# A transformer layer with 32 experts on one core: the maxima's transposes move to another PSUM room, VectorE gets a written order in the attention, and TensorE a written order with five batches of transposes in the experts

## The chip, the core and the metric

The kernel runs on one core of one Trainium2 chip. The metric is the device time of one execution in microseconds (us); of several executions the median is compared. Engines are TensorE (PE in the profile, with PEld for its weight loads), VectorE (DVE), ScalarE (ACT), GpSimd (POOL) and SyncE (SP, which issues most DMAs here).

## What is computed

One layer on a sequence of 1024 positions and width 1024: grouped-query attention (16 query heads of 64, 4 key/value heads, so four query heads share a group), then LayerNorm, then a mixture of 32 experts of which each token takes four, then LayerNorm.

```python
def query_block(q_blk):                       # 128 queries
    s = jnp.einsum('bqkgd,bskd->bkgqs', q_blk, k).astype(jnp.float32) * scale
    p = jax.nn.softmax(s, axis=-1).astype(v.dtype)
    return jnp.einsum('bkgqs,bskd->bqkgd', p, v)
...
def clamped_swiglu(h):
    h_glu = jnp.minimum(h[..., 0::2], SWIGLU_LIMIT)
    h_lin = jnp.clip(h[..., 1::2], -SWIGLU_LIMIT, SWIGLU_LIMIT)
    return h_glu * jax.nn.sigmoid(SWIGLU_ALPHA * h_glu) * (h_lin + 1.0)
...
def expert_block(args):                       # 128 rows of one expert
    xblk, e = args
    h = xblk @ w_gate_up[e] + b_gate_up[e]
    return clamped_swiglu(h) @ w_down[e] + b_down[e]
...
x = layer_norm(DEEPNORM_ALPHA * x + h, ln_mix_g[i], ln_mix_b[i])
f = moe_ffn(x, ...)                           # top 4 of 32, weighted by gates
x = layer_norm(DEEPNORM_ALPHA * x + f, ln_ffn_g[i], ln_ffn_b[i])
```

## The kernel before, in words

Everything is in 32-bit floats. A product that must be exact is made from a high and a low part of its operands: ScalarE casts the high part, VectorE subtracts it from the whole to get the low part, and TensorE adds three products.

**Attention.** The loop has 32 iterations n, of a query block i (0 to 7) and a group g (0 to 3), n = 4i + g, and in each eight steps k over blocks of 128 keys. In one step TensorE makes the transposed scores of its own iteration in two matmuls (`st<-qs,kT_hi` and `st<-q,kT_lo`), which ScalarE turns into `pt` by exp, and one matmul `sc` of the scores of iteration n + 2, of which only the maxima are wanted: VectorE reduces each pair of them (`nm<-sc`). Those four columns of negative maxima are transposed by TensorE (`tpm`, in `maxima_a`) and multiplied by VectorE into four rows of the operand `q2` (`q<-tpm,ident`), so that the second `st` matmul subtracts the maxima; ScalarE copies the rest of that operand (`maxima_b`). At k = 3 TensorE also makes the values' product of iteration n - 1 (`po`, 32 narrow matmuls, in `pv`). GpSimd adds up six of the eight `pt` of an iteration (`acc`), VectorE the last (`late_sum`). In iterations g = 1 and 2 the next block's queries are transposed in front of `po` (`tpq`, in `stack_q`, with two casts by ScalarE and two subtractions by VectorE). Once a block the sums are brought together (`su`), VectorE takes the reciprocal and spreads it (`rs`, `rh`, `rr`, all in `scale_a`), and two matmuls `rb` with two multiplications `ot<-ot,rb` scale the block's result (`scale_b`).

In PSUM `st` and `sc` have two rooms each, `po` one (`ps_o`), and all of `tpm`, `tpq`, `su` and `rb` share one (`ps_t`, tag `tp`): whoever writes it next waits until the one before has been read. TensorE runs in the order in which the code is written (`manual_schedule`); VectorE, ScalarE and GpSimd get their order from a scheduler when the kernel is built. Each engine runs its own list from front to back.

**Experts.** Expert e has eight gate/up chunks of 12 matmuls (`gu`, in `gate_up(e)`) and then the four down chunks of the expert before (`yp`, in `down(e-1)`). Each chunk's weights come by DMA, are cast by ScalarE (`wh`) and subtracted by VectorE (`wl`), in three rooms each: the cast of a chunk starts when TensorE has read the chunk three before it. Eighteen experts (1 to 8, and the even ones from 10 to 28) have room for 32 more rows: `go` in two batches of 32 matmuls, after chunk 3 and chunk 7, and `yq` at the end of the down product. Between chunks TensorE transposes what the next products need: `tpa` (two batches of four) and `tpao` (two transposes) for the down product of expert e - 1, and `tpx` (two batches of four) and `tpxo` (two) for expert e + 1, through one PSUM room again (`tp`); ScalarE and VectorE read it out (`xTh`, `xTl`, `aTh`, `aTl`, `xoT`, `aoT`). After `gate_up(e)` the activation is made: VectorE two `act<-gu`, ScalarE the silu, VectorE two `lin<-gu` and one `act<-lin,act`. Matmuls that only open a product with the bias (`gu<-b,sel`, `go<-b,sel`) depend on no weights. Only inside the down product of an expert with extra rows is TensorE's order the written one; elsewhere the scheduler may move its work. The loop that places the transposes:

```python
if e > 0:
    for part in range(3):
        between[part] = lambda part=part: turn_a(e - 1, part)
if e + 1 < NE:
    ...
        for part in range(3):
            between[(4 if e == 2 else 3) + part] = lambda part=part: turn_x(e + 1, part)
```

## Time and profile before

| | |
|---|---|
| time, three runs | 2078.68, 2079.25, 2081.83 us; median 2079.25 us |
| the profiled execution | 2075.34 us, of which the span from first to last instruction is 2073.5 us |
| granted TensorE clock, mean | 0.991 |
| busy share of the span | PE 97%, DVE 77%, ACT 62%, POOL 26% |
| stages of the span (us) | attention's loop 162.1 to 514.8; experts 633.5 to 2029.3 |

Busy shares are means over stages with different limits. TensorE is near its full share in both stages, so what a change is worth shows in TensorE's waits there, and in those that the change adds. An instruction's duration contains its start-up and write-out, so neighbours on one engine overlap a little; the distance from start to start is what it costs the engine.

### The profile page before, as it was taken

To read this page: it belongs to the slowest core of one execution; us is meant where nothing else is said; L and a number is where in the kernel's file an instruction comes from. 1 tells how busy PE (TensorE), PEld (TensorE's weight loads), DVE (VectorE), ACT (ScalarE), POOL (GpSimd) and SP (SyncE) were. 2 spreads that over 40 slices of the span, in tenths; PEclk is the share of its full clock that TensorE was granted. 3 is DMA by queue.
4 is the path that set the end of the run, shared out by engine and by line. 5 is a ranking of instruction groups with operands and counts; after the bars stand their busy time and mean duration, and the time that the engine had idled before them with its cause. 6 is when DMAs were issued, how large, how long until landed. Compare 5 with 4: busy or idle time off the path is not lost. (4 is left out here: it accounts for less than half of the span.)

```text
span 2073.5 us, 28716 instructions
## 1 busy us (share of the span) xinstructions
PE 2011.8 (97%) x10691; PEld 1419.5 (68%) x10691; DVE 1601.8 (77%) x1649; ACT 1282.0 (62%) x1566; POOL 538.2 (26%) x373
## 2 busy tenths in 40 slices
PE   8998999999997999999999999999999999999997
PEld 6775666665675666666666767767777677677774
DVE  6647777776887877767777878878878788887894
ACT  5655655654554656566666766667667676676774
POOL 1216777775144211111102111101021121010100
PEclk9999999999998999999999999999999999999999
DMA  5216000000645777888788898978989889789875
GB/s 174 72 62 178 31 32 21 32 21 21 228 149 211 276 287 271 298 294 291 285 315 312 347 338 304 377 289 342 338 319 354 310 315 367 284 346 337 329 314 183
DMA packets 106352, 500.44 MB, mean 241 GB/s; under 512 B 16001, under 2 KB 17026, under 8 KB 73442
## 3 DMA queue, kind: packets, MB, share of 16 engines
q1 hardware_dynamic: 87360, 447.02, 56.0%
q0 software_dynamic: 16000, 50.90, 9.0%
q8 instruction: 85, 1.39, 0.3%
q10 hardware_dynamic: 2850, 0.66, 0.2%
q14 instruction: 57, 0.47, 0.1%
HBM read 457.05 MB, written 41.49 MB: 240 GB/s over the span
## 5 line engine op out<-in xcount | busy, mean ns | idle before, releaser
L55 PE MATMUL gu<-wh,xTh 128*128 128x512 f32 x1024 | 415.3, 406 | 1.0 <-ACT xTh L63 1.0
L55 PE MATMUL gu<-wh,xTl 128*128 128x512 f32 x1024 | 410.1, 400 | 0.0
L55 PE MATMUL gu<-wl,xTh 128*128 128x512 f32 x1024 | 401.9, 393 | 0.0
L1299 POOL DMA_INDIRECT fd<-y,mi x32 | 79.1, 2472 | 655.4 <-ACT y L1298 655.4
L448 POOL TENSOR_TENSOR acc<-acc,pt 128x512 f32<-128x512 f32 x152 | 211.8, 1394 | 78.3 <-ACT pt L444 68.7
L55 PEld LDWEIGHTS gu<-wh,xTh 128*128 128x128 f32 x1024 | 193.3, 189 | 42.4 <-ACT xTh L63 1.7
L55 PEld LDWEIGHTS gu<-wl,xTh 128*128 128x128 f32 x1024 | 193.3, 189 | 39.6 <-issue 0.2
L55 PEld LDWEIGHTS gu<-wh,xTl 128*128 128x128 f32 x1024 | 193.7, 189 | 38.8 <-issue 3.6
L55 PE MATMUL yp<-wl,aTh 128*128 128x512 f32 x512 | 204.2, 399 | 0.4 <-DVE wl L612 0.4
L55 PE MATMUL yp<-wh,aTh 128*128 128x512 f32 x512 | 201.6, 394 | 0.0
L55 PE MATMUL yp<-wh,aTl 128*128 128x512 f32 x512 | 199.7, 390 | 0.0
L434 DVE TENSOR_REDUCE nm<-sc 128x1 fp32r<-128x1024 f32 x124 | 150.6, 1221 | 50.5 <-PE sc L55 49.5
L444 ACT ACTIVATE pt<-st 128x512 f32<-128x512 f32 x256 | 149.4, 596 | 55.9 <-PE st L55 46.3
L598 POOL DMA_INDIRECT xg<-xd,mi x32 | 53.4, 1670 | 298.5 <-PE tpx L1136 288.9
L55 PE MATMUL qkv<-wh,xT 128*128 128x512 f32 x384 | 123.9, 403 | 2.6 <-ACT xT L63 1.4
L55 PEld LDWEIGHTS yp<-wh,aTh 128*128 128x128 f32 x512 | 96.2, 188 | 33.6 <-ACT act L1180 14.3
L55 PE MATMUL po<-pt,vn 128*64 128x256 f32 x1024 | 117.6, 382 | 0.0
L55 PE MATMUL st<-qs,kT_hi 128*128 128x512 f32 x256 | 112.5, 440 | 2.9 <-ACT pt L444 2.2
L55 PEld LDWEIGHTS yp<-wl,aTh 128*128 128x128 f32 x512 | 96.3, 188 | 21.9 <-DVE wl L612 1.2
L55 PEld LDWEIGHTS yp<-wh,aTl 128*128 128x128 f32 x512 | 96.1, 188 | 19.5
L55 PE MATMUL st<-q,kT_lo 128*128 128x512 f32 x256 | 102.2, 399 | 1.3 <-DVE q L148 1.3
L55 PE MATMUL sc<-kT_hi,qs 128*128 128x512 f32 x256 | 101.9, 404 | 1.0 <-DVE nm L434 0.8
(520 smaller groups left out, 4159.0 us busy)
## 6 DMA issues: line engine op xcount, KB each, us to landing
w0g<-in_expert_w_gate_up SPq DMA_DIRECT2D x8, 1024.0 KB, 7.1
w1g<-in_expert_w_gate_up SPq DMA_DIRECT2D x8, 1024.0 KB, 7.6
w2g<-in_expert_w_gate_up SPq DMA_DIRECT2D x8, 1024.0 KB, 9.6
w3g<-in_expert_w_gate_up SPq DMA_DIRECT2D x8, 1024.0 KB, 8.6
w4g<-in_expert_w_gate_up SPq DMA_DIRECT2D x8, 1024.0 KB, 6.9
w5g<-in_expert_w_gate_up SPq DMA_DIRECT2D x8, 1024.0 KB, 7.4
w6g<-in_expert_w_gate_up SPq DMA_DIRECT2D x8, 1024.0 KB, 6.5
w7g<-in_expert_w_gate_up SPq DMA_DIRECT2D x8, 1024.0 KB, 7.1
```

Of the source, the lines that this page charges most:

```text
L55: nc.tensor.matmul(o, lhsT=lhsT, rhs=rhs, start=start, stop=stop)
L434: nc.vector.tensor_reduce(nms[n][:, m:m + 1], sc.pop((n, m)), AX.X, ALU.max, negate=True)
L444: nc.scalar.activation(pts[n, k], st, AF.Exp)
L448: (nc.vector if n == NG - 1 or n == NG - 2 and k > 3 else nc.gpsimd).tensor_tensor(accs[n], pts[n, 0] if k == 1 else accs[n], pts[n, k], A ...
L598: return nc.gpsimd.indirect_dma_start(out=xg[e], out_offset=None, in_=xd, in_offset=bass.IndirectOffsetOnAxis(ap=mi[:, e:e + 1] if rows is ...
L1299: nc.gpsimd.indirect_dma_start(out=fd, out_offset=bass.IndirectOffsetOnAxis(ap=mi[:, e:e + 1], axis=0), in_=y, in_offset=None, bounds_chec ...
```

## The change

*Attention.* `tpm` is written into the room of the values (`ps_o`, tag `po`, of which `po` now takes half), and from iteration 1 on at k = 5 rather than k = 2. `late_sum` stands behind `stack_q` and `maxima_b`. The multiplication `rr` leaves `scale_a` and becomes `scale_c`, at k = 7 of g = 0. `scale_b` moves from g = 1 (k = 5 and 7) to g = 3 (k = 1 and 5) of the same block. VectorE too runs in the written order in this loop.

*Experts.* From after `gate_up(1)` to the end TensorE runs in the written order. The transposes stand behind chunks 0 and 2 (`tpa`), 4 (new `turn_o`: `tpxo` and `tpao` as one batch in one room) and 5 and 7 (`tpx`), rather than 0, 1, 2 and 3, 4, 5. The bias of `go` is opened just before its first batch.

```diff
-    def maxima_a(n, ps):
-
-        tp = ps.tile([P, 4, P], F32, tag="tp", name=f"tpm{n}")
+    def maxima_a(n, tp):
+
...
         def pv(n):
...
-            po[n] = ps_o.tile([P, 2, P], F32, tag="po", name=f"po{n}")
+            po[n] = ps_o.tile([P, 4, P], F32, tag="po", name=f"po{n}")
...
             nc.vector.scalar_tensor_tensor(rs, hi.bitcast(F32), low, rs, ALU.mult, ALU.subtract)
+            rrs[i] = rs
+
+        def scale_c(i):
+            rs = rrs[i]
...
-        pe_order.enter_context(tc.manual_schedule(engines={mybir.EngineType.PE}))
+        pe_order.enter_context(tc.manual_schedule(engines={mybir.EngineType.PE, mybir.EngineType.DVE}))
...
-                if k == (6 if n == 0 else 2) and n + 1 < NG:
-                    maxima_a(n + 1, ps_t)
+                if k == (6 if n == 0 else 5) and n + 1 < NG:
+
+                    maxima_a(n + 1, ps_o.tile([P, 4, P], F32, tag="po", name=f"tpm{n + 1}"))
...
-                if k == (7 if n == 0 else 3) and n + 1 < NG:
+                if n == 0 and k == 7:
                     maxima_b(n + 1)
+                if k == 7 and g == 0 and 0 < n < NG:
+                    scale_c(i - 1)
                 if k == 3 and n > 0:
                     if g in (1, 2) and i + 1 < NT:
                         stack_q(i + 1, g - 1, ps_t)
+                    if n + 1 < NG:
+                        maxima_b(n + 1)
                     if n < NG - 1:
                         late_sum(n - 1)
...
-                    if (g, k) == (1, 5) or n == NG and k == 5:
+                    if (g, k) == (3, 1) or n == NG and k == 5:
                         scale_b(i - 1, 0)
-                    if (g, k) == (1, 7) or n == NG and k == 7:
+                    if (g, k) == (3, 5) or n == NG and k == 7:
                         scale_b(i - 1, 1)
...
+        def turn_o(e):
+
+            tp = ps_t.tile([P, 4, P], F32, tag="tp", name=f"tpo{e}")
+            if e + 1 < NE and ovf(e + 1):
+                for c in range(2):
+                    nc.tensor.transpose(tp[:, 2 + c, :], xo[e + 1][:, c * P:(c + 1) * P], ident)
+                xoT[e + 1] = mp.tile([P, 2, P], F32, tag="xoT", bufs=2, name=f"xoT{e + 1}")
+                nc.scalar.copy(xoT[e + 1], tp[:, 2:4, :])
+            if ovf(e - 1):
+                for c in range(2):
+                    nc.tensor.transpose(tp[:, c, :], acto[e - 1][:, c * P:(c + 1) * P], ident)
+                nc.scalar.copy(actoT[e - 1], tp[:, 0:2, :])
...
-            for n in range(4 if ovf(e) else 0):
-                mm(go[n * OVF:(n + 1) * OVF], sel[:, e:e + 1].to_broadcast([P, OVF]),
-                   b3[:, n * 512:(n + 1) * 512], True, False)
...
                 if k % 4 == 4 - 1:
+                    for n in range(4 if ovf(e) and k == 4 - 1 else 0):
+                        mm(go[n * OVF:(n + 1) * OVF], sel[:, e:e + 1].to_broadcast([P, OVF]),
+                           b3[:, n * 512:(n + 1) * 512], True, False)
...
-            in_turn = ExitStack()
-            if ovf(e):
-                in_turn.enter_context(tc.manual_schedule(engines={mybir.EngineType.PE}))
...
+            elif e > 1:
+                between[0] = lambda: turn_a(e - 1, 0)
+                between[2] = lambda: turn_a(e - 1, 1)
+                between[4] = lambda: turn_o(e)
...
-                    for part in range(3):
-                        between[(4 if e == 2 else 3) + part] = lambda part=part: turn_x(e + 1, part)
+                    for k, part in zip((5, 7) if e > 1 else (3, 4, 5), range(3)):
+                        between[k] = lambda part=part: turn_x(e + 1, part)
...
             if e == 1:
                 list_blocks()
+
+                in_turn.enter_context(tc.manual_schedule(engines={mybir.EngineType.PE}))
```

How the rows stand on the engines, before and after, at three places. Names carry numbers here: `sc23_1` is the second score matmul pair of iteration 23, `acc22` the sums of iteration 22.

TensorE in the attention, iteration 21 (block 5, g = 1), steps 2 and 3, before:

```order
L147 MATMUL tpm22_3692<-ident_70,nm22_3577 4x128
L55 MATMUL st21_2_3695<-qs5_3305,kT_hi_105 128x512
L55 MATMUL st21_2_3695<-q2_0_112,kT_lo_106 128x512
L55 MATMUL sc23_1_3701<-kT_hi_105,qs5_3305 128x512
L55 MATMUL st21_3_3703<-qs5_3305,kT_hi_105 128x512
L55 MATMUL st21_3_3703<-q2_0_112,kT_lo_106 128x512
L55 MATMUL sc23_1_3701<-kT_hi_105,qs5_3305 128x512
L163 MATMUL tpq6_0_3713<-ident_70,ql6_3666 128x128 x4
L55 MATMUL po20_3725<-pt20_0_3565,vn_107 64x256 x2
```

TensorE in the same iteration, step 4's end to step 6, with the change:

```order
L55 MATMUL sc23_2_3747<-kT_hi_105,qs5_3301 128x512
L146 MATMUL tpm22_3749<-ident_70,nm22_3577 4x128
L55 MATMUL st21_5_3752<-qs5_3301,kT_hi_105 128x512
L55 MATMUL st21_5_3752<-q2_0_112,kT_lo_106 128x512
L55 MATMUL sc23_2_3747<-kT_hi_105,qs5_3301 128x512
L55 MATMUL st21_6_3760<-qs5_3301,kT_hi_105 128x512
```

The transpose `tpm22` has left the place ahead of step 2, where the room is then taken by `tpq6_0`, and stands between steps 4 and 5, behind the values' product.

VectorE at the end of block 5's first iteration (n = 20) and into the next, before:

```order
L452 TENSOR_TENSOR acc23_3885<-acc23_3885,pt23_7_3963 128x512
L434 TENSOR_REDUCE nm26_3982<-sc26_0_3973 128x1
L148 TENSOR_TENSOR q2_1_1558<-tpm25_3984,ident_70 4x512
L434 TENSOR_REDUCE nm26_3982<-sc26_1_3993 128x1
L479 RECIPROCAL rs5_4040<-su5_4023 128x128
L481 CAST rh5_4042<-rs5_4040 128x128
L482 SCALAR_TENSOR_TENSOR rs5_4040<-rh5_4042,low_122,rs5_4040 128x128
L434 TENSOR_REDUCE nm26_3982<-sc26_2_4053 128x1
L484 TENSOR_TENSOR rr5_4045<-rs5_4040,col_120 128x1024
L434 TENSOR_REDUCE nm26_3982<-sc26_3_4069 128x1
L434 TENSOR_REDUCE nm27_4095<-sc27_0_4086 128x1
```

The same stretch with the change (`late_sum` is `acc23`, the reciprocal's chain `rs5`, `rh5`, `rr5`):

```order
L433 TENSOR_REDUCE nm26_3982<-sc26_0_3973 128x1
L433 TENSOR_REDUCE nm26_3982<-sc26_1_3990 128x1
L451 TENSOR_TENSOR acc23_3878<-acc23_3878,pt23_7_3963 128x512
L478 RECIPROCAL rs5_4037<-su5_4020 128x128
L480 CAST rh5_4039<-rs5_4037 128x128
L481 SCALAR_TENSOR_TENSOR rs5_4037<-rh5_4039,low_122,rs5_4037 128x128
L147 TENSOR_TENSOR q2_1_1558<-tpm25_4050,ident_70 4x512
L433 TENSOR_REDUCE nm26_3982<-sc26_2_4048 128x1
L433 TENSOR_REDUCE nm26_3982<-sc26_3_4067 128x1
L487 TENSOR_TENSOR rr5_4078<-rs5_4037,col_120 128x1024
L433 TENSOR_REDUCE nm27_4095<-sc27_0_4086 128x1
```

The multiplication into `q2` has moved behind the reciprocal's chain, `late_sum` behind the two reductions, and `rr5` behind the last reduction of the iteration.

VectorE around the end of the gate/up product of expert 15, which has no extra rows (`wl184` to `wl187` are the four down chunks of expert 14; `xTl_16` comes from the transposes `tpx16`), before:

```order
L64 TENSOR_TENSOR xTl_16_11546<-tpx16_0_11548,xTh_16_11545 128x512
L612 TENSOR_TENSOR wl183_11584<-w15g7_11394,wh183_11582 128x2048
L64 TENSOR_TENSOR xTl_16_11546<-tpx16_1_11573,xTh_16_11545 128x512
L612 TENSOR_TENSOR wl184_11606<-w14d0_11412,wh184_11604 128x2048
L1179 TENSOR_SCALAR act15_11440<-gu15_0_11434 128x512
L612 TENSOR_TENSOR wl185_11624<-w14d1_11442,wh185_11622 128x2048
L1179 TENSOR_SCALAR act15_11440<-gu15_1_11435 128x512
L1183 TENSOR_SCALAR lin15_11441<-gu15_0_11434 128x512
L1183 TENSOR_SCALAR lin15_11441<-gu15_1_11435 128x512
L612 TENSOR_TENSOR wl186_11657<-w14d2_11470,wh186_11655 128x2048
L1185 SCALAR_TENSOR_TENSOR act15_11440<-lin15_11441,act15_11440 128x1024
L612 TENSOR_TENSOR wl187_11675<-w14d3_11495,wh187_11673 128x2048
```

VectorE at the same place with the change:

```order
L622 TENSOR_TENSOR wl184_11564<-w14d0_11378,wh184_11562 128x2048
L64 TENSOR_TENSOR xTl_16_11552<-tpx16_0_11553,xTh_16_11551 128x512
L1202 TENSOR_SCALAR act15_11406<-gu15_0_11400 128x512
L622 TENSOR_TENSOR wl185_11582<-w14d1_11408,wh185_11580 128x2048
L1202 TENSOR_SCALAR act15_11406<-gu15_1_11401 128x512
L64 TENSOR_TENSOR xTl_16_11552<-tpx16_1_11596,xTh_16_11551 128x512
L1206 TENSOR_SCALAR lin15_11407<-gu15_0_11400 128x512
L1206 TENSOR_SCALAR lin15_11407<-gu15_1_11401 128x512
L622 TENSOR_TENSOR wl186_11620<-w14d2_11436,wh186_11618 128x2048
L1208 SCALAR_TENSOR_TENSOR act15_11406<-lin15_11407,act15_11406 128x1024
L622 TENSOR_TENSOR wl187_11638<-w14d3_11454,wh187_11636 128x2048
```

The first `xTl_16` now stands behind `wl184` and the second behind both `act15`, ahead of `lin15`, `wl186` and `wl187`.

ScalarE at the same place, before:

```order
L63 CAST xTh_16_11545<-tpx16_0_11548 128x512
L607 CAST wh183_11582<-w15g7_11394 128x2048
L63 CAST xTh_16_11545<-tpx16_1_11573 128x512
L607 CAST wh184_11604<-w14d0_11412 128x2048
L1138 COPY xoT16_11547<-tpxo16_11598 128x256
L607 CAST wh185_11622<-w14d1_11442 128x2048
L607 CAST wh186_11655<-w14d2_11470 128x2048
L1180 ACTIVATE act15_11440<-act15_11440 128x1024
L607 CAST wh187_11673<-w14d3_11495 128x2048
```

ScalarE with the change:

```order
L617 CAST wh183_11535<-w15g7_11360 128x2048
L1187 COPY xoT16_11528<-tpo15_11525 128x256
L1191 COPY aoT14_11428<-tpo15_11525 128x256
L617 CAST wh184_11562<-w14d0_11378 128x2048
L63 CAST xTh_16_11551<-tpx16_0_11553 128x512
L617 CAST wh185_11580<-w14d1_11408 128x2048
L617 CAST wh186_11618<-w14d2_11436 128x2048
L63 CAST xTh_16_11551<-tpx16_1_11596 128x512
L1203 ACTIVATE act15_11406<-act15_11406 128x1024
L617 CAST wh187_11636<-w14d3_11454 128x2048
```

The second cast `xTh_16` now stands behind the cast `wh186`, and the copies `xoT16` and `aoT14` follow each other.

## Rows read from the trace of the kernel before

**Rows 1.** Busy time by stretch: the attention's steady part, experts 4 to 28.

```profile
core 0: us, PE busy (x) PEld busy (x) DVE busy (x) ACT busy (x) POOL busy (x), PEclk, DMA share, GB/s
...
201.00:497.00 296.00, 284.70 (x1826) 185.39 (x1826) 229.24 (x228) 171.54 (x307) 223.64 (x163) 1.00 0.09 32
...
820.00:1949.00 1129.00, 1129.00 (x5931) 799.70 (x5930) 902.47 (x613) 740.71 (x536) 167.34 (x80) 1.00 0.85 320
```

**Rows 2.** TensorE's waits, 201 to 497 us: total, times, longest.

```profile
PE tpq L163 <- DVE q L148: 4.1, 12, 0.5
PE tpm L147 <- DVE nm L434: 3.9, 7, 0.6
PE rb L55 <- DVE ot L492: 2.7, 7, 0.4
```

**Rows 3.** TensorE's waits, 160 to 201 us.

```profile
PE tpq L163 <- DVE q L148: 3.2, 2, 2.8
```

**Rows 4.** Busy time by stretch: the four iterations of block 5.

```profile
386.92:397.81 10.89, 10.89 (x91) 7.16 (x90) 8.82 (x10) 5.44 (x10) 7.99 (x7) 1.00 0.01 2
397.81:410.13 12.32, 11.12 (x65) 7.27 (x64) 10.31 (x11) 8.09 (x15) 9.98 (x7) 1.00 0.01 1
410.13:420.90 10.77, 10.25 (x62) 6.68 (x61) 7.66 (x9) 6.69 (x12) 7.08 (x7) 1.00 0.28 99
420.90:430.92 10.02, 9.96 (x58) 6.41 (x58) 7.25 (x6) 5.55 (x10) 7.99 (x7) 1.00 0.01 2
sum 44.00, PE 42.22 PEld 27.51 DVE 34.06 ACT 25.77 POOL 33.05; mean PE 10.55 PEld 6.88 DVE 8.51 ACT 6.44 POOL 8.26
```

**Rows 5.** Timeline of VectorE in block 5's first iteration: start, duration.

```profile
389.55 1.76 DVE L452 TENSOR_TENSOR acc<-acc,pt 128x512 f32<-128x512 f32 x1 [1.20 <-POOL acc L448]
...
392.48 0.68 DVE L148 TENSOR_TENSOR q<-tpm,ident 4x512 fp32r<-4x512 f32 x1
...
394.94 0.96 DVE L479 RECIPROCAL rs<-su 128x128 f32<-128x128 f32 x1 [0.53 <-PE su L55]
...
396.51 1.22 DVE L434 TENSOR_REDUCE nm<-sc 128x1 fp32r<-128x1024 f32 x1
397.65 1.21 DVE L484 TENSOR_TENSOR rr<-rs,col 128x1024 fp32r<-128x1024 f32 x1
```

**Rows 6.** Timeline of TensorE, block 5's second iteration into its third.

```profile
406.09 0.50 PE L55 MATMUL st<-qs,kT_hi 128*128 128x512 f32 x1
...
406.89 0.40 PE L55 MATMUL st<-qs,kT_hi 128*128 128x512 f32 x1
...
410.13 0.39 PE L55 MATMUL st<-qs,kT_hi 128*128 128x512 f32 x1
...
410.83 0.39 PE L55 MATMUL st<-qs,kT_hi 128*128 128x512 f32 x1
```

**Rows 7.** Timeline of VectorE, expert 15's activation and expert 14's down weights.

```profile
1347.76 0.68 DVE L1179 TENSOR_SCALAR act<-gu 128x512 f32<-128x512 f32 x1
1348.36 1.28 DVE L1183 TENSOR_SCALAR lin<-gu 128x512 f32<-128x512 f32 x2
1349.55 2.28 DVE L612 TENSOR_TENSOR wl<-w14d,wh 128x2048 fp32r<-128x2048 f32 x1
1351.75 1.22 DVE L1185 SCALAR_TENSOR_TENSOR act<-lin,act 128x1024 f32<-128x1024 f32 x1
1352.89 2.28 DVE L612 TENSOR_TENSOR wl<-w14d,wh 128x2048 fp32r<-128x2048 f32 x1
```

**Rows 8.** Timeline of ScalarE, the same stretch.

```profile
1339.41 0.59 ACT L63 CAST xTh<-tpx 128x512 fp32r<-128x512 f32 x1 [0.46 <-PE tpx L1136]
...
1342.41 0.37 ACT L1138 COPY xoT<-tpxo 128x256 f32<-128x256 f32 x1 [0.16 <-PE tpxo L1136]
...
1346.08 1.91 ACT L607 CAST wh<-w14d 128x2048 fp32r<-128x2048 f32 x1 [0.82 <-PE gu L55]
```

**Rows 9.** Timeline of TensorE, the same stretch: transposes between chunks and inside one.

```profile
1333.63 0.39 PE L55 MATMUL gu<-wl,xTh 128*128 128x512 f32 x1
1333.87 0.60 PE L1136 MATMUL tpx<-ident,xg 128*128 128x128 f32 x4
...
1334.53 0.40 PE L55 MATMUL gu<-wh,xTl 128*128 128x512 f32 x1
...
1338.43 0.39 PE L55 MATMUL gu<-wh,xTh 128*128 128x512 f32 x1
...
1339.45 0.40 PE L55 MATMUL gu<-wl,xTh 128*128 128x512 f32 x1
```

**Rows 10.** Timeline of TensorE, expert 14's down product.

```profile
1346.11 0.39 PE L55 MATMUL yp<-wh,aTh 128*128 128x512 f32 x1
...
1351.77 0.39 PE L55 MATMUL yp<-wh,aTl 128*128 128x512 f32 x1
...
1352.04 0.58 PE L55 MATMUL yp<-wl,aTh 128*128 128x512 f32 x1
```

More of the change, by code (lines that the diff above doesn't have):

```diff
@@ L348, in trunk_kernel @@
                 if i == NT - 1 and k == 6:
-                    maxima_a(0, ps1)
+                    maxima_a(0, ps1.tile([P, 4, P], F32, tag="tp", name="tpm0"))
                     maxima_b(0)
@@ L456, in pv @@
             i, g = divmod(n, NKV)
-            po[n] = ps_o.tile([P, 2, P], F32, tag="po", name=f"po{n}")
+            po[n] = ps_o.tile([P, 4, P], F32, tag="po", name=f"po{n}")
             for k in range(NT):
                 for a in range(2):
-                    mm(po[n][a * HD:(a + 1) * HD].rearrange("p j t -> p (j t)"), vn[:, k, g, :],
+                    mm(po[n][a * HD:(a + 1) * HD, 0:2, :].rearrange("p j t -> p (j t)"), vn[:, k, g, :],
                        pts[n, k][:, 2 * a * P:(2 * a + 2) * P], k == 0, k == NT - 1)
@@ L468, in close_a @@
                 ot[i] = p2.tile([P, KD, P], F32, tag="ot", bufs=2, name=f"ot{i}")
-            nc.scalar.copy(ot[i][:, 2 * g:2 * g + 2, :], po.pop(n))
+            nc.scalar.copy(ot[i][:, 2 * g:2 * g + 2, :], po.pop(n)[:, 0:2, :])
         def scale_a(i):
@@ L553, in trunk_kernel @@
                         scale_a(i - 1)
+                    if n == NG:
+                        scale_c(i - 1)
                 if i > 0:
-                    if (g, k) == (1, 5) or n == NG and k == 5:
+                    if (g, k) == (3, 1) or n == NG and k == 5:
                         scale_b(i - 1, 0)
-                    if (g, k) == (1, 7) or n == NG and k == 7:
+                    if (g, k) == (3, 5) or n == NG and k == 7:
                         scale_b(i - 1, 1)
@@ L1144, in turn_x @@
                 xT[e] = [mx.tile([P, KD, P], F32R, tag=f"xT{a}", bufs=2, name=f"xT{a}_{e}") for a in "hl"]
-                if ovf(e):
+                if ovf(e) and e < 3:
                     xoT[e] = mp.tile([P, 2, P], F32, tag="xoT", bufs=2, name=f"xoT{e}")
@@ L1269, in down @@
             later = []
-            in_turn = ExitStack()
-            if ovf(e):
-                in_turn.enter_context(tc.manual_schedule(engines={mybir.EngineType.PE}))
             for c in range(KD // 2):
@@ L1296, in down @@
                     between[c]()
-            in_turn.close()
             nc.scalar.mul(y, yp, gm_s[:, e:e + 1])
@@ L1318, in trunk_kernel @@
         fetch(8)
+        in_turn = ExitStack()
         for e in range(NE):
             between = {}
-            if e > 0:
+            if e == 1:
                 for part in range(3):
                     between[part] = lambda part=part: turn_a(e - 1, part)
+            elif e > 1:
+                between[0] = lambda: turn_a(e - 1, 0)
+                between[2] = lambda: turn_a(e - 1, 1)
+                between[4] = lambda: turn_o(e)
             if e + 1 < NE:
@@ L1344, in trunk_kernel @@
         down(NE - 1)
+        in_turn.close()
     es_w.close()
```

## The prediction, made before the changed kernel ran

> **What bounds the kernel now.** I read the busy time by stretch first. From 820 to 1949 us, in the middle of the experts, TensorE is busy for 1129.00 of 1129.00 us; from 201 to 497 us, in the attention, for 284.70 of 296.00 [rows 1]. So both stages are bound by TensorE: in the experts only its own work can shrink or a new wait be added, in the attention there are 11.3 us of idling to win back. The list of waits, read next, names them: 4.1 us for `tpq` behind `q`, 3.9 for `tpm` behind the reductions, 2.7 for `rb` behind `ot`, together 10.7 in 26 waits [rows 2], and 3.2 before the steady part [rows 3]. All three are transposes or matmuls that want the one room `tp` or VectorE's last result. Cut by iteration, a block takes 44.00 us, of which TensorE works 42.22; 1.20 of the idle 1.78 lies in the second iteration (12.32 against 11.12), 0.52 in the third, almost none in the others [rows 4].
>
> **The attention's waits go.** With the change `tpm` no longer takes the room just ahead of `tpq`, so `tpq` waits for no `q`; the room of the values is free by then, since `po` has been copied out two steps before k = 5. `rb` moves to the fourth iteration, where VectorE is least loaded (7.25 us in 10.02, against 10.31 in 12.32 in the second, [rows 4]) and where nothing else wants the room. All of the 13.9 us [rows 2, 3] is then up for removal: the operations are the same in number and size, they only stand elsewhere. Not all of it comes back. A step that follows a stall takes 0.70 us (410.13 to 410.83), one that follows none 0.80 (406.09 to 406.89) [rows 6], because during the stall ScalarE's exp catches up and frees the rooms of `st`. A removed stall so costs up to 0.10 in the next step. Twenty-eight waits by 0.10 is 2.8 at most, nothing at least; I take 1.9, since some stalls stand where the next step would have been short anyway. Attention: 13.9 - 1.9 = **-12.0 us**, bounds -11.1 and -13.9.
>
> **What VectorE's written order could add there.** The tightest place is the first iteration of a block, begun at S = 386.92 in the trace. Now `q` runs early, at 392.48 [rows 5]; with the change it stands behind the reciprocal, which began 8.0 after S, at 394.94, and waited only for `su` [rows 5]. Reciprocal, cast and correction take 1.57 to the next reduction at 396.51; then `q` for 0.68 ends about 10.2 after S. The next iteration begins 10.9 after S and needs `q` in its second matmul, at 11.1: 0.9 to spare. Behind `q` stand two reductions of 1.22 and `rr` of 1.21 [rows 5], which reach about 2.7 us into the next iteration, where the next reduction's scores are ready after 1.8. It starts 0.9 late, and whom does that delay? The score matmuls of that iteration's fifth step, which need the room, and those come only after the values' product, over 3 us later. The one near thing is the first score matmul of the new iteration, which needs the room that the third reduction frees at about the same moment: up to 0.1 a block, 0.7 in all. I count it at nothing, for the cover of a free second room, and hold 0.7 for the range.
>
> Where the sums of one iteration are finished (`late_sum`), VectorE took 1.76 us for 512 columns, though `rr` beside it needed 1.21 for 1024 [rows 5], so something held it for about 1.1 us (1.76 less the 0.68 that `q` takes for 512 columns). In the written order it stands behind the second reduction, which ends some 4.5 after S; even at 1.76 it ends at 6.3, and `su`, which needs it, comes at about 6.8 (1.1 us of `su` and its latency before the reciprocal). 0.5 to spare, and no term. The Trainium skill (SBUF — State Buffer, "Who interferes with whom") says that a VectorE instruction with two SBUF inputs and a GpSimd one that reads SBUF exclude each other for a whole instruction, and that the one that starts first wins. By that rule the 1.76 is a wait for a GpSimd addition, the trace's two durations agree, and each moved `late_sum` or `rr` may be held once more; it is the first rival below, which the sum does without.
>
> **The experts: cheaper transposes.** A batch of four transposes between two chunks costs 0.90 from the matmul ahead to the second one behind (1333.63 to 1334.53); inside a chunk's triple it costs 1.02 (1338.43 to 1339.45) [rows 9]. With two matmuls of 0.23 taken off, that is 0.44 and 0.56. In the written order all batches stand between chunks. An expert with extra rows whose neighbours have them too (2 to 8) has three batches inside chunks now and one batch more than after: 3 x 0.12 and about half of 0.44 for the small batch, -0.55, by seven = -3.9. The ten even ones from 10 to 28 gain two moves of 0.12 and about 0.1 for the bias of `go`, which no longer splits a triple: -0.35 by ten = -3.5. The eleven odd ones from 9 and expert 30 gain about 0.2 each: -2.4. Sum -9.8.
>
> **The experts: a new wait.** In those twelve the down weights arrive just in time. Before, `wl` of the third down chunk ended at 1349.55 + 2.28 = 1351.83 [rows 7], and TensorE took it at 1352.04 [rows 10]: 0.21 of slack, part of it because the scheduler had put a bias matmul of the next expert in front. With the change three things alter. First, four transposes stand at the end of the gate/up product, so the down product starts 0.44 later, at 1346.55. Its matmuls run 0.2264 apart (25 from 1346.11 to 1351.77 [rows 10]), and the bias is gone from among them, so the first `wl` of chunk three is wanted 26 matmuls on, at 1352.44. Second, ScalarE casts `xTh` only behind the `wh` that ran from 1346.08 to 1347.99, and takes 0.59 for it [rows 8]: 1348.6. Third, VectorE's `xTl` (0.68) waits for that and stands ahead of `lin`, so `lin` begins at 1349.3 instead of 1348.36 [rows 7], and both `wl` come 0.9 later: the third is done at 1352.7, a wait of 0.3; the fourth ends at 1352.89 + 2.28 + 0.9 = 1356.1, when TensorE, 0.3 late, wants it at 1352.7 + 12 x 0.2264 = 1355.4: another 0.7. I take 0.9 for both (the third wait is near the resolution of the sum), by twelve = +10.8. The bounds are nothing, if the cast slips in before `wh`, and twice as much. Behind the waiting matmul stands all of TensorE's work, and the next expert's casts have 2 us and more of slack by the same shift, so the wait doesn't grow. Experts: -9.8 + 10.8 = **+1.0**, from -9.8 to +11.8.
>
> **The sum.** -12.0 + 1.0 = -11.0 on the profiled execution's 2075.34, which gives 2064.3. That execution lies 3.9 below the median of the runs (2079.25), and I carry the difference over: 2068.2, rounded to 2068. A change of 0.2% is 4.2 us, about what a measurement of this kernel tells from no change.
>
> **Rivals.** (1) *The port gives half of it back.* If `late_sum` in a block's first iteration is held by two additions rather than one, it ends 1.1 later, 0.6 after `su` wants it, and `q` is then 0.2 past its slack less what TensorE lost with it; with the same in the second and third iteration, whose `tpq` subtractions now stand ahead of it, about 1.1 a block, 8 us over seven: 2076. For it: GpSimd works 33.05 of a block's 44.00 us [rows 4], so an addition is nearly always running. Against: one hold is already counted, and rooms for four scores lie between.
> (2) *The experts' waits don't come.* ScalarE's casts are then in time and only the -9.8 counts: 2079.25 - 12.0 - 9.8 = 2057.5. For it: before, the same weights met TensorE with 0.21 to spare and no wait in 1129 us. Against: the rows of VectorE's and ScalarE's order are fixed, and both put the late cast ahead.
> (3) *They come twice as long*, since the wait delays the activation, which delays the fourth `wl` again: +10.8 more, 2079, no change.
> (4) *Slower: the transposes' room.* `turn_o` after chunk 4 is emptied by two copies of 0.37, which stand behind a cast of 1.91 that starts when the chunk is read [rows 8]: 2.7 us after it. The next batch wants the room one chunk and one batch later, 12 x 0.2264 + 0.44 = 3.2. In the written order TensorE can't go around it. If the copies came behind one cast more, it would wait about 1.4 in each of the 17 experts that have both copies (3 to 8, odd 9 to 29), +24 us: 2092. It ends slower than now from 0.9 us of wait each (15.2 / 17 = 0.9 for 4.2 beyond no gain). Against: the order of ScalarE puts both copies directly behind the cast, 0.5 in time.
>
> **Chances.** My forecast, within 5 us: 0.60. (1) 0.12, (2) 0.13, (3) 0.09, (4) 0.06. The predicted time is 2068. Leaving (4) and the outer half of (2) and (3) out gives 2058 to 2078. Faster by over 0.2% (below 2075.1): the forecast, (2) and half of (1): 0.79; within 0.2%: the other half and (3): 0.14; slower: 0.07.
>
> **What would show it.** In the attention: no `tpq`, `tpm` or `rb` among TensorE's waits, a block in about 42.6 us with the second iteration near 10.6 and the fourth near 10.4. If (1) holds, `su` or `st` behind VectorE appear there. In the experts: `yp` behind `wl`, 24 waits of 0.2 to 0.7, all in the odd experts' stretch; pairs of experts then take about as long as now, single ones 0.5 less. If (4) holds, `tpx` behind ScalarE's `xoT` or `aoT`. The prediction is wrong if a block still takes 43.5 us or the waits in the experts sum to over 15.

## The result: 2092.5 us, slower, outside the range

The changed kernel took 2092.5 us (median of four, 2091.18 to 2094.04) against 2078.97 in the same comparison (2077.38 to 2081.83): a ratio of 1.0064, 95% interval 1.0046 to 1.0081. Forecast were 2068 us, from 2058 to 2078, and 0.07 for slower. The two halves of the change went opposite ways, and TensorE's waits in the profile after show both. In the attention, 201 to 490 us, the three lines of [rows 2] are gone, and one stands there that was not there before: TensorE now waits for ScalarE's exp (waiter, releaser: total, times, longest):

```profile
PE st L55 <- ACT pt L443: 1.2, 7, 0.2
```

In the experts, 820 to 1949 us, where TensorE waited for nothing before, there are now two:

```profile
PE tpo L1190 <- ACT xoT L1187: 25.4, 14, 1.8
PE yp L55 <- DVE wl L622: 3.1, 10, 0.3
```

The four iterations of block 5, to be held against [rows 4], with the columns as there:

```profile
375.55:386.54 10.99, 10.96 (x91) 7.20 (x90) 7.70 (x10) 5.46 (x10) 7.85 (x7) 1.00 0.13 50
386.54:396.90 10.36, 10.32 (x62) 6.66 (x62) 9.82 (x10) 7.34 (x13) 8.60 (x7) 1.00 0.01 2
396.90:407.39 10.49, 10.32 (x63) 6.81 (x62) 7.66 (x9) 7.34 (x13) 7.66 (x7) 1.00 0.14 52
407.39:417.65 10.26, 10.26 (x60) 6.76 (x60) 7.32 (x9) 5.56 (x10) 8.18 (x7) 1.00 0.00 0
sum 42.10, PE 41.87 PEld 27.42 DVE 32.51 ACT 25.70 POOL 32.29; mean PE 10.47 PEld 6.86 DVE 8.13 ACT 6.42 POOL 8.07
```

A block went from 44.00 to 42.10 us, and the first expert's product began at 617.5 us instead of 633.5. From there to the end of the last down product it took 1428.7 us instead of 1396.0. So the attention gave 16.0 and the experts took 32.7, together 16.7; the span grew by 16.6 (2073.5 to 2090.1). The granted clock was 0.992 against 0.991, so it has no part in this.

The wait on `tpo` is inside `turn_o` itself. TensorE after chunk 4 of expert 15 (start, duration, engine, line, operation):

```profile
1336.77 0.39 PE L55 MATMUL gu<-wl,xTh 128*128 128x512 f32 x1
1336.99 0.38 PE L1185 MATMUL tpo<-ident,xo 128*128 128x128 f32 x2
1339.19 0.44 PE L1190 MATMUL tpo<-ident,acto 128*128 128x128 f32 x2 [1.81 <-ACT xoT L1187]
1339.38 0.48 PE L55 MATMUL gu<-wh,xTh 128*128 128x512 f32 x1
```

And ScalarE at the same time:

```profile
1336.96 1.90 ACT L617 CAST wh<-w15g 128x2048 fp32r<-128x2048 f32 x1 [0.80 <-PE gu L55]
1338.77 0.37 ACT L1187 COPY xoT<-tpo 128x256 f32<-128x256 f32 x1
1339.66 0.37 ACT L1191 COPY aoT<-tpo 128x256 f32<-128x256 f32 x1 [0.53 <-PE tpo L1190]
```

Both pairs of transposes write one room, and `turn_o` asks for the copy of the first pair before it asks for the second pair. The second pair therefore waits until the room has been read; that copy stands behind a cast of 1.90 us which starts when chunk 4 has been read, that is, at the very moment at which the transposes do. It waits although it writes another half of the room (`tp[:, 0:2]`; the copy reads `tp[:, 2:4]`). TensorE, in the written order, has nothing it may do meanwhile: 1.81 us.

Sixteen experts have both pairs (2 to 7 and the odd ones from 9 to 27), and the wait stands in all of them: 14 times in the list above, twice before 820 us. There expert 2 has 6.5 us of it, because ScalarE's queue waits 4.59 us for a DMA (`bt<-ebi`) ahead of the copy. The list of waits has 33.8 us on `tpo` in all.

### The profile page after: what moved, and what is told of

The parts are those of the page before. It is cut to its first block, busy times and chain, and to the rows that moved or that the text cites. A ratio compares the mean times of both kernels' runs of the same rounds, so it can differ in the third digit from the quotient of the medians.

```text
span 2090.1 us, 28694 instructions
## 1 busy us (share of the span) xinstructions
PE 2006.3 (96%) x10691; PEld 1423.9 (68%) x10691; DVE 1589.3 (76%) x1649; ACT 1275.7 (61%) x1566; POOL 543.8 (26%) x373
## 5 line engine op out<-in xcount | busy, mean ns | idle before, releaser
L55 PE MATMUL gu<-wh,xTl 128*128 128x512 f32 x1024 | 401.0, 392 | 0.0
L447 POOL TENSOR_TENSOR acc<-acc,pt 128x512 f32<-128x512 f32 x152 | 200.4, 1318 | 70.5 <-ACT pt L443 60.9
L608 POOL DMA_INDIRECT xg<-xd,mi x32 | 62.1, 1941 | 437.4 <-PE tpx L1146 429.2
L55 PEld LDWEIGHTS yp<-wl,aTh 128*128 128x128 f32 x512 | 96.1, 188 | 34.5 <-DVE wl L622 14.8
```

What stands on the lines that cost most here:

```text
L55: nc.tensor.matmul(o, lhsT=lhsT, rhs=rhs, start=start, stop=stop)
L447: (nc.vector if n == NG - 1 or n == NG - 2 and k > 3 else nc.gpsimd).tensor_tensor(accs[n], pts[n, 0] if k == 1 else accs[n], pts[n, k], A ...
L608: return nc.gpsimd.indirect_dma_start(out=xg[e], out_offset=None, in_=xd, in_offset=bass.IndirectOffsetOnAxis(ap=mi[:, e:e + 1] if rows is ...
```

## The experiments

All are compared with the kernel before, run beside them. A ratio stands with its 95% interval. Where two changed kernels of different comparisons are set against each other, the difference of their medians is given; the kernel before read 2077.2 to 2079.0 us in those comparisons, so about 2 us of such a difference can be noise.

**The two halves apart.** In `e1_attention_only` the code ahead of the experts is the changed one, the experts' the old; `e2_experts_only` is the reverse.

> The attention's part of the change alone, the experts as before. If the two parts add up, as the stages of the trace say (the experts' stage begins 16.0 us earlier, at 617.5 instead of 633.5): 2079 - 16 = 2063 us. If the attention's gain is partly lent by the experts (weights that come later against the earlier start of the experts): 2070 or more.

Measured: 2060.54 us, 0.9921 (0.9904 to 0.9937). The attention's gain is not lent by the experts.

> The experts' part alone, the attention as before. If the parts add up: 2079 + 29.5 = 2108 us, with about 34 us of TensorE's waits on the copy xoT between the two pairs of transposes in turn_o. If the loss comes from the experts starting earlier than their weights: about 2079 to 2085.

Measured: 2111.7 us, 1.0163 (1.0147 to 1.018), with 34.1 us of waits on the copy in 16 times. This is close to the theory. The halves add up within the noise: -16.65 and (2111.7 against 2077.19) +34.5 make +17.9, the whole change measured +13.5, and each interval reaches 3.5 us to either side. The stages of the whole change's trace gave -16.0 and +32.7.

**What in `turn_o` waits.** In `e3_copies_behind_all_four` the two copies are written behind both pairs:

```diff
                 for c in range(2):
                     nc.tensor.transpose(tp[:, 2 + c, :], xo[e + 1][:, c * P:(c + 1) * P], ident)
-                xoT[e + 1] = mp.tile([P, 2, P], F32, tag="xoT", bufs=2, name=f"xoT{e + 1}")
-                nc.scalar.copy(xoT[e + 1], tp[:, 2:4, :])
             if ovf(e - 1):
                 for c in range(2):
                     nc.tensor.transpose(tp[:, c, :], acto[e - 1][:, c * P:(c + 1) * P], ident)
+            if e + 1 < NE and ovf(e + 1):
+                xoT[e + 1] = mp.tile([P, 2, P], F32, tag="xoT", bufs=2, name=f"xoT{e + 1}")
+                nc.scalar.copy(xoT[e + 1], tp[:, 2:4, :])
+            if ovf(e - 1):
                 nc.scalar.copy(actoT[e - 1], tp[:, 0:2, :])
```

> The whole change, but turn_o issues all four transposes first and then both copies. Theory: the two pairs share one room, so the second pair waits until ScalarE has copied the first, and that copy stands behind a cast of 1.91 us; without it the 34 us of waits go and the time is about 2060 us, with the waits on wl in the odd experts' stretch growing from 0.64 each to 0.9. Rival: ScalarE itself is late there, so the wait moves to the next transposes (tpx), which need the same room, and the time stays above 2080 us.

Measured: 2060.83 us, 0.992 (0.9903 to 0.9936). Moving the copies gives 31.7 us (29.9, if each of the two kernels is taken against the kernel before of its own comparison). In fifteen of the sixteen experts the wait did not go on to the next batch; in expert 2, where a DMA holds ScalarE, 4.0 us of it stand at `tpx` now. Expert 15's transposes, TensorE again:

```profile
1319.27 0.38 PE L1185 MATMUL tpo<-ident,xo 128*128 128x128 f32 x2
1319.49 0.38 PE L1188 MATMUL tpo<-ident,acto 128*128 128x128 f32 x2
1319.63 0.48 PE L55 MATMUL gu<-wh,xTh 128*128 128x512 f32 x1
...
1322.47 0.60 PE L1146 MATMUL tpx<-ident,xg 128*128 128x128 f32 x4
```

and ScalarE empties the room at 1321.31 + 0.38 = 1321.69, 0.8 before `tpx` wants it:

```profile
1321.05 0.36 ACT L1191 COPY xoT<-tpo 128x256 f32<-128x256 f32 x1
1321.31 0.38 ACT L1193 COPY aoT<-tpo 128x256 f32<-128x256 f32 x1
```

In `e4_six_batches` the pairs get a turn of the room each, `xo` after chunk 3 and `acto` after chunk 4:

```diff
...
-                between[4] = lambda: turn_o(e)
+                between[3] = lambda: turn_o(e, 0)
+                between[4] = lambda: turn_o(e, 1)
```

> The whole change, but xo after chunk 3 and acto after chunk 4, each as its own batch in its own turn of the room: six batches in the written order. Theory: no wait between the pairs, but one batch more in every expert with extra rows: about 2064 us. Rival (ScalarE is late): the wait shows at the acto batch or at tpx, above 2080 us.

Measured: 2076.27 us, 0.9997 (0.9987 to 1.0006). Neither number: the wait between the pairs is gone, and another stands in its place, 820 to 1900 us:

```profile
PE tpxo L1146 <- DVE aTl L64: 15.1, 10, 1.5
PE yp L55 <- DVE wl L622: 3.2, 10, 0.3
```

The batch after chunk 3 comes one chunk after `tpa`, whose room VectorE has not read yet. So the room can be late for any batch that follows too closely, as the rival said, but not in the place where it named it. One chunk of 2.7 us between two batches is enough for a cast and two copies by ScalarE (e3); it is not enough for a cast, the cast of `aTh`, and VectorE's `aTl` behind a subtraction `wl` of 2.29.

In `e11_without_written_order` the change's `turn_o` stays as it is, and TensorE's written order is taken back to where it was (only in the down product of experts with extra rows):

```diff
...
             if e == 1:
                 list_blocks()
-
-                in_turn.enter_context(tc.manual_schedule(engines={mybir.EngineType.PE}))
```

> The whole change with turn_o as it is, but TensorE's written order in the experts taken back to where it was before (only inside the down product of experts with extra rows). The scheduler then puts ten matmuls of a weight chunk between the two pairs of turn_o (the order shows it). Theory (a wait of 1.8 us on the copy that lies between the pairs, which the written order exposes): the 34 us go without turn_o being changed, about 2060 us. Rival (the room itself is late, so any order waits): above 2080 us.

Measured: 2051.84 us, 0.9872 (0.9855 to 0.989), 40.7 below the changed kernel, 8.7 below the attention's part alone, and 8 below the theory's 2060. The scheduler lets nine matmuls through between the pairs (the expectation counted ten):

```profile
1316.42 0.38 PE L1185 MATMUL tpo<-ident,xo 128*128 128x128 f32 x2
1316.55 0.47 PE L55 MATMUL gu<-wh,xTh 128*128 128x512 f32 x1
...
1318.72 0.38 PE L1190 MATMUL tpo<-ident,acto 128*128 128x128 f32 x2
1318.86 0.48 PE L55 MATMUL gu<-wh,xTh 128*128 128x512 f32 x1
```

So the 1.81 us needs both: a read between two writes of one room, and an order that lets nothing past. The 8 us beyond the theory go with the waits on `wl`. None of those is listed here from 820 to 1900 us, although VectorE's order is the changed one: the scheduler has put bias matmuls of the next expert ahead of the late weights, as it had before (there one and two of them).

```profile
1331.90 0.39 PE L55 MATMUL gu<-b,sel 128*128 128x512 bf16 x1
1332.06 0.50 PE L55 MATMUL yp<-wl,aTh 128*128 128x512 f32 x1
...
1334.92 0.82 PE L55 MATMUL gu<-b,sel 128*128 128x512 bf16 x3
1335.40 0.57 PE L55 MATMUL yp<-wl,aTh 128*128 128x512 f32 x1
```

**The waits on the down weights.** `e5_second_batch_late` is e3 with the second batch of `tpx` behind the last down chunk:

```diff
-                    for k, part in zip((5, 7) if e > 1 else (3, 4, 5), range(3)):
+                    for k, part in zip((5,) if e > 1 else (3, 4, 5), range(3)):
...
+            elif e > 1:
+                down(e - 1, {3: lambda: turn_x(e + 1, 1)})
```

> The kernel of the copies behind all four transposes (2060.8 us), with the second batch of tpx not behind chunk 7 but behind the last chunk of the down product. Theory: the waits on wl (0.17 and 0.47 us in the eleven odd experts' stretch and those of expert 30, 4.2 us by the list of waits, about 7.7 us by the distance of the matmuls) come from xTh and xTl standing ahead of wl; they go, and the time is about 2053 us. Rival: the missing bias matmuls, which stood inside the down product before, gave the weights their time; then most of the wait stays, 2059 to 2061 us.

Measured: 2065.39 us, 0.9947 (0.9929 to 0.9965), slower than e3. The theory fell: the waits on `wl` stay (3.0 us in ten, 3.2 in e3, 820 to 1900 us), as the rival said, though not with its time. Measured from the last gate/up matmul, the third `wl` does start 0.76 earlier (3.67 us after it instead of 4.43). But with the four transposes gone from that place the down product starts 0.35 earlier as well, and ahead of the fourth `wl` VectorE still makes two `lin` and the last product: the third chunk's wait goes, the fourth's stays. And the transposes, now just ahead of the next `tpa`, make that one wait (6.4 us in ten). VectorE in `e3_copies_behind_all_four`, where the last gate/up matmul starts at 1328.15 and the down product at 1328.73:

```profile
1330.77 0.69 DVE L64 TENSOR_TENSOR xTl<-tpx,xTh 128x512 fp32r<-128x512 f32 x1
1331.38 1.28 DVE L1208 TENSOR_SCALAR lin<-gu 128x512 f32<-128x512 f32 x2
1332.58 2.28 DVE L622 TENSOR_TENSOR wl<-w14d,wh 128x2048 fp32r<-128x2048 f32 x1
1334.78 1.22 DVE L1210 SCALAR_TENSOR_TENSOR act<-lin,act 128x1024 f32<-128x1024 f32 x1
1335.91 2.28 DVE L622 TENSOR_TENSOR wl<-w14d,wh 128x2048 fp32r<-128x2048 f32 x1
```

`e9_lin_behind_weights` therefore leaves `tpx` where the change put it and moves `lin` and the last product, in experts without extra rows, behind the second down chunk:

```diff
...
-            def whole():
+            def whole(late=None):
...
                 nc.scalar.activation(a, a, AF.Silu, scale=SW_A)
+                if late is not None:
+                    late.append(rest)
+                else:
+                    rest()
+
+            def rest():
                 for i in range(n):
...
-                whole()
+                whole(late_act if e > 1 and not ovf(e) else None)
...
-                down(e - 1)
+                down(e - 1, {1: lambda: late_act.pop()()} if late_act else {})
```

> The kernel of the copies behind all four transposes (2060.8 us), with lin and the last product of the activation written after the second down chunk in experts without extra rows, so that VectorE makes both wl first. Theory (VectorE's queue of activation work ahead of wl is what makes TensorE wait): wl of the third and fourth down chunk come 1.2 to 1.8 us earlier, no wait on wl is left in the odd experts' stretch, 40.52 goes to about 39.9 us, and the time is about 2054 us. Rival (the casts of ScalarE are late): 2060 us.

Measured: 2049.64 us, 0.9866 (0.985 to 0.9883), 11.2 less than e3. VectorE now has, at the same place:

```profile
1327.58 0.69 DVE L64 TENSOR_TENSOR xTl<-tpx,xTh 128x512 fp32r<-128x512 f32 x1
1328.19 2.28 DVE L622 TENSOR_TENSOR wl<-w14d,wh 128x2048 fp32r<-128x2048 f32 x1
1330.39 0.68 DVE L1214 TENSOR_SCALAR lin<-gu 128x512 f32<-128x512 f32 x1
1330.99 2.28 DVE L622 TENSOR_TENSOR wl<-w14d,wh 128x2048 fp32r<-128x2048 f32 x1
```

and TensorE waits for nothing from 820 to 1900 us. The down product starts at 1325.54 here, so the third and fourth `wl` come 2.65 and 5.45 us after its start instead of 3.85 and 7.18 in e3: 1.2 and 1.7 earlier, as foretold. ScalarE's casts were not late. The time is 4 us below the theory's 2054. In `e10_bias_in_down` e3's bias matmuls for the next expert stand behind the second down chunk instead, about where the scheduler had put some of them before:

```diff
...
-                down(e - 1)
+                down(e - 1, {1: lambda: open_gu(e + 1)} if e > 1 and not ovf(e) else {})
```

> The kernel of the copies behind all four transposes (2060.8 us), with the four bias matmuls of the next expert behind the second chunk of the down product of experts with extra rows ahead of which no such expert's product ran, as the scheduler had put some of them before. Theory (those matmuls were the time that the weights needed): about 0.9 us of work stands ahead of the third chunk, no wait on wl is left, about 2054 us. Rival: VectorE's chain only shifts and the fourth chunk waits still, 2058 us.

Measured: 2053.99 us, 0.9888 (0.9871 to 0.9904), and no wait on `wl` in the list. Both cures work: give VectorE the time, or take work out of its way. So the wait had two conditions, VectorE's work ahead of `wl` and the missing bias matmuls. What keeps e10 4.4 us above e9 is open; 1.7 of it lies in experts 9 to 30 of the traces.

`e12_lin_without_written_order` takes the written order back from e9, as e11 did from the change.

> The best kernel so far (2049.6 us) with the same taken back. If the written order is worth the 0.12 us by batch that the rows of before show (three batches in six experts, about two in the others): 2053 to 2056 us. If it is worth nothing by itself: 2050 us.

Measured: 2048.49 us, 0.9855 (0.9838 to 0.9873). From the first expert to 1970 us the two traces have TensorE's matmuls in the same order, and behind that they differ in two places; so the 1.1 us between e9 and e12 is about what two measurements of the same TensorE order differ by. It has the lowest median of the study, 30.5 us below the kernel before and some 44 below the changed one; the written order gave nothing to it.

**The attention's parts**, each with the experts as before. `e6_room_alone` has only `tpm` in the values' room at k = 5, with VectorE's order left to the scheduler; `e7_written_order_alone` only VectorE's written order; `e8_rb_in_its_old_place` is e1 with `scale_b` back at g = 1:

```diff
# e6
...
-                if k == (6 if n == 0 else 2) and n + 1 < NG:
-                    maxima_a(n + 1, ps_t)
+                if k == (6 if n == 0 else 5) and n + 1 < NG:
+                    maxima_a(n + 1, ps_o.tile([P, 4, P], F32, tag="po", name=f"tpm{n + 1}"))
# e7
-        pe_order.enter_context(tc.manual_schedule(engines={mybir.EngineType.PE}))
+        pe_order.enter_context(tc.manual_schedule(engines={mybir.EngineType.PE, mybir.EngineType.DVE}))
# e8, against e1
-                    if (g, k) == (3, 1) or n == NG and k == 5:
+                    if (g, k) == (1, 5) or n == NG and k == 5:
...
-                    if (g, k) == (3, 5) or n == NG and k == 7:
+                    if (g, k) == (1, 7) or n == NG and k == 7:
```

> The experts and VectorE's order as before; of the attention's part only the room of tpm (values' room, at k = 5). Theory: the room is what mattered, the waits of tpq (4.1 + 3.2 us) and tpm (3.9) go and those of rb (2.7) stay: 2077 - 11 = 2066 us. Rival: without the written order VectorE's late additions still hold what comes behind, and half of it stays: 2071 us.

> The kernel before, with VectorE in the written order in the attention and nothing else. Theory (the room matters): the multiplication into q2 stands where it stood, the waits stay, 2074 to 2080 us. Rival (the order is what mattered): 2068 us or less.

> The attention's part alone (2060.5 us), but scale_b back in the second iteration of the block. Theory: that iteration's wait for rb comes back, about 0.4 us a block, and VectorE has 10.3 us of work in about 10.4: 2063 to 2066 us. Rival: without tpm in the same room rb waits for nothing, 2060.5 us.

Measured: e6 2065.86 us, 0.9948 (0.9931 to 0.9964); e7 2079.95, 1.0009 (1.0 to 1.0019); e8 2063.38, 0.9928 (0.9912 to 0.9945). All three came out by their theories. In e6 the waits of `tpq` and `tpm` are gone, `rb` still waits (1.7 us in six, 201 to 480 us), and `sc` behind `nm` has come (2.0 in five), of which the rival spoke; in e8 `rb` alone of these is left (1.7 in six). Block 5 as one stretch, in e6, e8, e1 and e7 (length, then the engines' busy times as in [rows 4]):

```profile
377.92:420.73 42.81, 41.92 (x271) 27.46 (x271) 34.16 (x35) 25.90 (x46) 32.30 (x25) 1.00 0.08 26
```

```profile
377.24:419.70 42.46, 41.94 (x271) 27.39 (x271) 32.76 (x35) 25.91 (x46) 32.37 (x25) 1.00 0.07 26
```

```profile
375.89:417.97 42.08, 41.85 (x271) 27.40 (x271) 32.54 (x35) 25.68 (x46) 32.30 (x25) 1.00 0.07 26
```

```profile
388.13:433.28 45.15, 42.42 (x271) 27.52 (x271) 32.84 (x34) 25.91 (x46) 32.21 (x25) 1.00 0.07 25
```

The room is worth 1.19 of the 1.92 us a block; the written order with `late_sum` and `rr` in their new places 0.35, `rb` in the fourth iteration 0.38. By the runs' medians the room gave 11.9 of 16.65 us. The written order on the old code makes a block longer, since `rr` then stands ahead of two reductions: there `sc` waits 7.6 us in six times for `nm` (longest 1.5). So the order pays only together with the rearranged code; that code without the order was not tried.

## Why the prediction was wrong, step by step

- **The failed step is `turn_o`, in "the experts: cheaper transposes".** The batch of `tpxo` and `tpao` was priced as one batch, "one batch more than after ... about half of 0.44". It is two pairs with a read of the same room between them, and the read stands behind a cast. The price is 31.7 us (e3 against the change). In expert 15 it is 2.03 us by the lines shown: 2.20 from the first pair to the second instead of 0.22, and 0.05 more behind them. The fourth rival named the room, the copies and the cast, and even came out at 2092, but for another mechanism: it had the next batch (`tpx`) wait for the room, and dismissed it on 0.5 us of spare time. That spare time was real (0.8 in e3). The wait was one step earlier, within the function, where the order of the copies in the diff shows it; the agreement of its number is chance (it also counted 17 experts with both pairs; there are 16). Its argument against, that both copies stand directly behind the cast, reads an order list as if neighbours followed each other in time: the second copy waited 0.53 us for its transposes. The forecast's own sign of being wrong came true: the waits on `tpo` and `wl` sum to some 37 us, over 15.
- **The other terms of the experts held.** Without the inner wait they were to give +1.0; e3 differs from e1 by +0.3. Apart: the cheaper transposes were put at -9.8, and e9, which has them and no waits (but also the moved `lin`), is 10.9 below e1; the wait on `wl` was put at 0.9 in each of twelve experts, +10.8, and e3 is 11.2 above e9 and 6.8 above e10. By distance, from the first down matmul of expert 9 to that of expert 27, nine pairs of experts take 753.1 us in e1, 753.5 in e3, 745.2 in e9 and 746.7 in e10: 0.93 or 0.76 a pair for the wait, and 0.88 or 0.72 a pair for the transposes, where 0.55 was put. In the changed kernel itself the wait showed as `yp` behind `wl`, as foretold, though the list has 13 such waits (one of them was there before) where 24 were foretold. The named cause was right in part: `xTl` delays `wl` by 0.76 of the forecast 0.9, but taking it away alone (e5) does not end the wait, and bias matmuls in the down product (e10, e11) end it with `xTl` where it is.
- **The attention was sized too small: -12.0, measured -16.65** (e1), beyond the bound of -13.9. All three kinds of wait went, as said, a block takes 42.1 us (foretold 42.6), the second iteration 10.36 (10.6) and the fourth 10.26 (10.4). Two sizes were off, against each other: the steps that don't stall grew by more than the deduction of 1.9 for exp, and the waits weigh more than the list of waits says, which outweighs it (the last section has both).
- **VectorE's written order added no wait**, as the sum had it. (The two lists of VectorE's order ahead of the prediction, headed n = 20, show n = 24: `rs5` closes block 5.) The first rival's mechanism did show: `rr` in block 5, which took 1.21 before [rows 5], took 1.94 in the changed kernel, where it starts while GpSimd's addition runs, and GpSimd's next addition took 2.25, where the same one took 1.28 before:

```profile
385.01 4.05 POOL L447 TENSOR_TENSOR acc<-acc,pt 128x512 f32<-128x512 f32 x3 [2.83 <-ACT pt L443]
388.20 1.94 DVE L487 TENSOR_TENSOR rr<-rs,col 128x1024 fp32r<-128x1024 f32 x1
389.01 2.25 POOL L447 TENSOR_TENSOR acc<-pt,pt 128x512 f32<-128x512 f32 x1
```

  Before, GpSimd paid instead: the three additions beside the `rr` of 1.21 took 4.99 us, the three ahead of it 4.01. That agrees with the Trainium skill's rule (SBUF — State Buffer, "Who interferes with whom"). `rr` so ended 3.6 us into the next iteration rather than the 2.7 of the forecast, and TensorE still waited for no reduction: the rival's price was not paid.
- **The second rival** ("the experts' waits don't come", 2057.5) describes e9 and e11 rather than the change, with the attention's larger gain on top. The third (waits twice as long) did not show: 0.93 a pair. In the chances the parts named for "within 0.2%" make 0.15 and not 0.14, those for slower 0.06 and not 0.07.

## What to carry to other kernels

When several writers share one PSUM room, read the code between two writes: a read that lies there turns one batch into two, and its price is whatever stands ahead of the reader on its engine, here a cast of 1.9 us. TensorE's written order in the experts gave nothing here that the scheduler's order didn't (e12), and it exposed both waits (e11); check each pair of neighbours in such an order for "who must have read this first". And where an engine prepares operands just in time, move its other work behind them: moving `lin` and the last product behind the two `wl` gave 11 us, as much as all the cheaper transposes.

## What the runs showed that I had not expected

A stall of TensorE costs more than the list of waits says. In the kernel before, `rb` with its wait:

```profile
408.98 0.40 PE L55 MATMUL sc<-kT_hi,qs 128*128 128x512 f32 x1
409.79 0.50 PE L55 MATMUL rb<-rr,half 128*128 128x512 f32 x1 [0.41 <-DVE ot L492]
410.13 0.39 PE L55 MATMUL st<-qs,kT_hi 128*128 128x512 f32 x1
410.36 0.40 PE L55 MATMUL st<-q,kT_lo 128*128 128x512 f32 x1
```

From `sc` to `rb` it is 0.81, where it is 0.23 when nothing waits. The list has 0.41 of that, because it counts from the end of `sc`, 0.40 after its start. Behind `rb` the next matmul starts 0.34 later instead of 0.23. The stall so costs 0.69 us where the list has 0.41. The wait in `turn_o` costs 2.03 where the list has 1.81. Where `wl` is late in e3, the list has 0.32 for the fourth chunk of expert 14:

```profile
1337.08 0.39 PE L55 MATMUL yp<-wl,aTh 128*128 128x512 f32 x1
...
1338.25 0.50 PE L55 MATMUL yp<-wl,aTh 128*128 128x512 f32 x1 [0.32 <-DVE wl L622]
...
1339.05 0.40 PE L55 MATMUL yp<-wl,aTh 128*128 128x512 f32 x1
```

Two matmuls that use `wl` are 0.68 apart when nothing waits; here it is 1.17, then 0.80. At the third chunk, whose wait the list does not have, it is 0.85 and 0.80. Together that is 0.90 us, the 0.9 of the forecast.

In the attention exp takes part of this back. With the change, in block 5:

```profile
398.15 0.40 PE L55 MATMUL sc<-kT_hi,qs 128*128 128x512 f32 x1
398.71 0.50 PE L55 MATMUL st<-qs,kT_hi 128*128 128x512 f32 x1 [0.17 <-ACT pt L443]
399.05 0.39 PE L55 MATMUL st<-q,kT_lo 128*128 128x512 f32 x1
```

Summed over block 5 from start to start, the steps into `tpm`, `tpq` and `rb` became 2.37 us shorter (the list had 1.72 there), the steps behind `tpm` and within `tpq` 0.58, and the steps into `st` and `sc` from one another 1.06 longer. That is the 1.9 us by which the block shrank. If all of the 1.06 is exp's, it is much more than the 1.9 that the forecast had for the whole loop; the list names exp for 0.17 of it, and the rest is not shown. All this is worked out from spacings, not tried by itself.
